# FFN of a two-layer trunk: two weight sums of a tile made one step earlier, SiLU and the gated product one step later

## The chip, the cores and the metric

The kernel runs on one core of one Trainium2 chip. Its time is the device time of one execution, in microseconds (us). The engines are TensorE (PE in the profile, with its weight loads as PEld), VectorE (DVE), ScalarE (ACT), GpSimd (POOL) and SyncE (SP), which here only issues DMAs. Each engine works through its own instructions strictly in the order in which they were written; an instruction that waits holds up all behind it on that engine.

## What is computed

A sequence of 1024 tokens of width 1024 passes two layers (a gated DeltaNet layer, then a chunked attention layer), each followed by the same kind of FFN, and a last norm. The change lies in the FFN:

```python
def conv_ffn(xn, w_up, conv_w, conv_b, w_down):
    h = causal_dwconv(xn @ w_up, conv_w) + conv_b
    gate, val = h[..., :FFN_DIM], h[..., FFN_DIM:]
    return (jax.nn.silu(gate) * val) @ w_down
```

FFN_DIM is 2816, the convolution has three taps along the sequence, and everything is in float32.

## The kernel before

**Matmuls.** A float32 product is made of three float32r matmuls: each operand is cut into a rounded high part (`h`) and the remainder, its low part (`l`), and high by high, low by high and high by low are added up in PSUM. A low part is always made in two pieces: ACT rounds (`cut_high`, L1379), then POOL or DVE subtracts (`cut_low`, through `tt`, L1358).

**Tiles of the first matrix.** `w_up` is taken in 22 tiles j of 128 gate columns and 128 value columns. With the contraction cut in halves, a tile is four blocks of weights: 11 and 12 (gate), 21 and 22 (value). It is multiplied in the manner of Strassen and Winograd: seven products of a sum of weight blocks with a sum of activation blocks, instead of eight. They run in the order 1, 7, 6, 5, 2, 4, 3. Products 1, 2 and 4 use the blocks 11, 12 and 22 as loaded. Four products need a sum of weight blocks first, made in place on DVE, each from the one before: 7: 21 = 11 − 21; 6: 21 = 21 − 22; 5: 11 = 21 + 11; 3: 12 = 12 − 21. In the profile such a sum is `r<-r,r` on DVE, the rounding is `uh<-r` on ACT, the low part `ul<-r,uh` on POOL. The activations are `x7` for product 7, `xt2` for 6, `xt1` for 5, `xt4` for 4, and `xh`, `xl` for 1, 2 and 3. The results are `pu` in PSUM. `after` (L1507 on) brings them to SBUF: `keep`, `vpre` and `gpre`.

**Convolution and gate.** `taps` makes the convolution of the value (v0, v1, v2) and of the gate (g0, g1, g2): the first tap on ACT (L1474), the two others on DVE (L1477, `val<-vpre,colt,val` and `gate<-gpre,colt,gate`). `silu` works on the gate in place on ACT (L1480, `gate<-gate`), `gated` multiplies the value by it in place on DVE (`val<-val,gate`). `hidden` cuts the result of tiles 18 to 20 into `hidh` (ACT) and `hidl` (DVE) for the last matmuls.

**The second matrix.** `w_down` is taken by nine groups g of two tiles, also by seven products each, in the order 1, 2, 5, 3, 6, 7, 4. Their weight parts are `dh` (ACT) and `dl` (POOL); the parts of the gated values ("channels") are `eh` (ACT) and `el` (DVE, or POOL in products 6 and 7). The results `pd` go to `stage` (copied by ACT, or added by DVE in products 6 and 7) and are sent to memory with an adding DMA from POOL's queue (`send`).

**The order.** All of it is written by hand. `step` appends to a list of PE steps; one step is one product, 12 matmuls. `at(i, f, rank)` puts a job ahead of step i, and the jobs of a step are emitted in order of rank. Results and `drain` have rank 0, sends 0.5, `operand` (sum, high and low part of a tile's product, two steps ahead of it) 1, the weights and channels of the second matrix (three steps ahead) 1.2 and 1.4, the convolution's pieces 2, loads 3. Two tiles and one group make 21 steps. With the products of the second matrix written d, an odd tile runs 1, 7, d5, 6, 5, d3, 2, 4, d6, 3 and an even tile 1, d7, 7, 6, d4, 5, 2, d1, 4, 3, d2. The list `when` gives the steps of the convolution: `nx(j, s)` is the s-th product of the tile after j.

```python
when[j] = [(pos[j, 7], (v0, v1), 2), (nx(j, 1), (v2, g0), 2), (nx(j, 2), (g1,), 2), (nx(j, 3), (g2, silu), 2), (nx(j, 4), (gated,), 2)]
```

Of the kernel before, what the change touches and what calls it, by code (L numbers as in the profile page):

```python
# [28 lines left out]
def trunk_kernel(  # L29
# [1323 lines left out]
    def ffn(layer, h, hp, xs, tail, d_r, last):  # L1353
# [19 lines left out]
        def at(i, f, rank=1):  # L1373

            jobs.setdefault(max(i, 0), []).append((rank, f))

        def cut_high(src, ring, copy=nc.scalar.copy):
            hi, lo = [(wd if ring == "e" else wf).tile([P, HALF], F32R, name=ring + x, tag=ring + x, bufs=RINGS[ring]) for x in "hl"]
            copy(hi, src)  # L1379
            return hi, lo  # L1380

        def cut_low(src, hi, lo, eng):
            tt(eng, lo, src, hi.bitcast(F32), sub)
# [44 lines left out]
        raw, ops = {}, {}  # L1428
# [8 lines left out]
            (nc.gpsimd if j == 0 else nc.sync).dma_start(out=t_, in_=w_up[k0 * P : (k0 + 4) * P, m * P : (m + 1) * P].rearrange("(k p) m -> p k m", p=P))  # L1437
            raw[j, q] = t_.rearrange("p k m -> p (k m)")

        def operand(j, n, lo=True):  # L1440

            a = lambda q: raw[j, q]
            if n == 7:
                tt(nc.vector, a(21), a(11), a(21), sub)
            elif n == 6:
                tt(nc.vector, a(21), a(22), a(21), sub)
            elif n == 5:
                tt(nc.vector, a(11), a(21), a(11), add)
            elif n == 3:
                tt(nc.vector, a(12), a(12), a(21), sub)  # L1450
            src = a({1: 11, 2: 12, 7: 21, 6: 21, 5: 11, 4: 22, 3: 12}[n])
            ops[j, n] = cut_high(src, "u")
            if lo:
                cut_low(src, *ops[j, n], nc.gpsimd)
            return lambda: cut_low(src, *ops[j, n], nc.vector)
# [51 lines left out]
        def after(j, n):  # L1507
            p_ = bank[j, {2: 1, 4: 7, 3: 5}.get(n, n)]
            if n == 1:
                keep[j] = tp.tile([P, HALF], F32, name="keep", tag="keep", bufs=2)  # L1510
                nc.scalar.copy(keep[j], p_)
            elif n == 6:
                tt(nc.vector, keep[j], p_, keep[j], add)
                keep[j, 7] = tp.tile([P, HALF], F32, name="keep7", tag="keep7")
                tt(nc.vector, keep[j, 7], bank[j, 7], keep[j], add)
            elif n == 5:
                tt(nc.vector, new_pre(j, 1)[:, HALF:SEQ], p_, keep[j, 7], add)
            elif n == 2:
                nc.scalar.copy(new_pre(j, 0)[:, 0:HALF], p_)
            elif n == 4:  # L1520
                tt(nc.vector, new_pre(j, 1)[:, 0:HALF], p_, keep[j], add)
            elif n == 3:
                tt(nc.vector, new_pre(j, 0)[:, HALF:SEQ], p_, keep[j], add)

        pos = {}
# [42 lines left out]
        end, fin_at = pos[FP - 1, 7], pos["d", NG - 1, 4]  # L1568
        early = pos["p", 1, 3]
        for i, (j, n) in due.items():  # L1570
            if i < early:
                low = []
                at(i - 2, lambda j=j, n=n, low=low: low.append(operand(j, n, False)), 1)
                at(i - 2, lambda low=low: low[0](), 2.5)
            else:
                at(i - 2, lambda j=j, n=n: operand(j, n), 1)
            if n != 2 or j > 2:
                at(i + 1, lambda j=j, n=n: after(j, n), 0)

        def nx(j, s):  # L1580
            return pos[j + 1, s] if j + 1 < FP else end + s
# [23 lines left out]
        for j in range(3, FP - 1):  # L1605
# [3 lines left out]
        v0, v1, v2, g0, g1, g2 = [(v, i) for v in (1, 0) for i in range(3)]  # L1609
        when = {  # L1610
            0: [(11, (g0,), 0), (12, (v0,), 0), (13, (v1,), 2), (13, (v2,), 2.7), (15, (g1, g2, silu), 2), (17, (gated,), 2)],
            1: [(18, (v0, v1), 2), (19, (v2, g0), 2), (20, (g1,), 2), (21, (g2, silu), 2), (22, (gated,), 2)],
            2: [(24, (v0, v1), 2), (25, (v2, g0), 2), (26, (g1,), 2), (27, (g2, silu), 2), (28, (gated,), 2)],
        }
        for j in range(3, FP - 1):
            when[j] = [(pos[j, 7], (v0, v1), 2), (nx(j, 1), (v2, g0), 2), (nx(j, 2), (g1,), 2), (nx(j, 3), (g2, silu), 2), (nx(j, 4), (gated,), 2)]
            if j >= 2 * NG:
                when[j].append(({18: fin_at + 5, 19: fin_at + 7}.get(j, max(nx(j, 5), fin_at + 9)), (hidden,), 1.9))
        for j, w_ in when.items():
            for i, fs, r in w_:  # L1620
                at(i, lambda j=j, fs=fs: [taps(j, *f) if isinstance(f, tuple) else f(j) for f in fs], r)
# [305 lines left out]
    d_h = [dram.tile([P, SEQ], F32, name=f"d_h{k}") for k in range(KT)]  # L1927
    xb = ([[None, None] for _ in range(KT)], [[None, None] for _ in range(KT)])
    ctx_f, tail0 = ffn(0, h, hp, normed, tails[0], d_r0, xb)
    ctx_o = ctx.enter_context(ExitStack())  # L1930
    wp = ctx_o.enter_context(tc.tile_pool(name="wp1", bufs=2, **SB))
# [288 lines left out]
    def norm_out(t, ht, fin):  # L2220
# [26 lines left out]
        return go()  # L2247

    ctx_f, _ = ffn(1, h, hp, normed, tails[0], d_r1, norm_out)
    ctx_f.close()  # L2250
    ctx_h.close()
# [56 lines left out]
```

## Time and profile before

| | us |
|---|---|
| median of three runs | 2642.77 |
| lowest and highest | 2642.44, 2644.0 |
| profiled execution | 2644.0 |
| its span, first to last instruction | 2642.0 |
| FFN of layer 0, steps of tiles | about 683 to 1314 of the span |
| FFN of layer 1, steps of tiles | about 1950 to 2584 of the span |

A row of a timeline has the start (us from the span's start), the duration, engine, line, operation and the tiles written and read; square brackets give the idle time of the engine just before and what ended it. An `x2` is two instructions told as one row. A row of the groups has busy time and mean ns, then the idle time ahead of the group and its releasers. Instructions of one engine follow each other with a little overlap in the records, and the busy time of a matmul contains its pipeline, so a row's duration is not always its price.

### The profile page before, as it was taken

How to read it: one execution, taken by the hardware profiler on the slowest of the kernel's cores; microseconds unless marked ns; L12 is line 12 of the kernel's file. 1: busy time of each engine (PE TensorE's matmuls, PEld its weight loads, DVE VectorE, ACT ScalarE, POOL GpSimd, SP SyncE). 2: the span in 40 equal slices, each digit the busy share in tenths (PEclk: the TensorE clock that was granted, in tenths of full speed). 3: DMA queues.
4: the chain of work that ended last, by engine and by line, in shares of the span. 5: the costliest groups of instructions: out<-in, count | busy, mean ns of one | idle time of the engine just before them, and what ended most of it. 6: DMA issues, size and time to landing. Idle time of an engine off the chain costs nothing.

```text
span 2642.0 us, 39392 instructions
## 1 busy us (share of the span) xinstructions
PE 2526.0 (96%) x13933; PEld 2069.7 (78%) x13933; DVE 1845.3 (70%) x3102; ACT 1409.1 (53%) x2714; POOL 1455.6 (55%) x1472
## 2 busy tenths in 40 slices
PE   7999899999999999999999999998999999999998
PEld 5878788888777777877778788887876778788776
DVE  5755765554678887888775666666478787777886
ACT  5444456464455555555455555555345555555543
POOL 3655553345347777777635444443343677777770
PEclk9999999999999999999999999999999999999999
DMA  4434335555337777777831111114232477777785
GB/s 127 137 100 121 117 105 156 159 162 160 89 88 150 141 148 151 144 143 152 191 128 50 43 58 45 45 47 143 89 95 76 132 147 141 150 147 150 151 192 176
DMA packets 317589, 326.71 MB, mean 124 GB/s; under 512 B 32976, under 2 KB 240592, under 8 KB 317392
## 3 DMA queue, kind: packets, MB, share of 16 engines
q1 hardware_dynamic: 285936, 219.07, 28.2%
q0 software_dynamic: 26560, 96.48, 20.9%
q10 hardware_dynamic: 4896, 8.65, 0.9%
q8 instruction: 109, 1.79, 0.3%
q14 instruction: 88, 0.72, 0.1%
HBM read 180.94 MB, written 143.20 MB: 123 GB/s over the span
## 4 chain that ended last, share of the span: by engine, by line
PE 47%; POOL 13%; issue 12%; DVE 12%; ACT 4%; DMA 2%; POOLq 0%; SPq 0%; ACTq 0%; DVEq 0%
POOL ul L1358 5%; PE pu L1393 5%; PE acc L120 4%; PE acc L121 4%; PE acc L122 4%; PE pu L1391 4%; PE pu L1392 4%; POOL dl L1358 3%; DVE r L1358 2%; DVE val L1477 2%; PE acco L120 2%; PE acco L122 2%; PE acco L121 2%; PE ptp L2058 2%; PE pd L1393 1%
## 5 line engine op out<-in xcount | busy, mean ns | idle before, releaser
L1358 POOL TENSOR_TENSOR ul<-r,uh 128x512 fp32r<-128x512 f32 x282 | 434.7, 1550 | 380.8 <-ACT uh L1379 362.1
L120 PE MATMUL acc<-xh,whi 128*128 128x512 f32 x896 | 376.2, 420 | 0.2 <-ACT xh L1097 0.2
L1379 ACT CAST uh<-r 128x512 fp32r<-128x512 f32 x296 | 179.9, 621 | 355.1 <-DVE r L1358 290.0
L121 PE MATMUL acc<-xl,whi 128*128 128x512 f32 x896 | 354.6, 396 | 1.6 <-POOL xl L379 1.0
L122 PE MATMUL acc<-xh,wlo 128*128 128x512 f32 x896 | 353.6, 395 | 0.6 <-POOL wlo L105 0.6
L105 POOL TENSOR_TENSOR wlo<-wraw,whi 128x256 fp32r<-128x256 f32 (+1 forms) x293 | 235.8, 836 | 199.4 <-ACT whi L103 158.2
L1393 PE MATMUL pu<-xh,ul 128*128 128x512 f32 x552 | 218.0, 395 | 16.9 <-POOL ul L1358 16.8
L1391 PE MATMUL pu<-xh,uh 128*128 128x512 f32 x552 | 216.0, 391 | 3.6 <-ACT uh L1379 2.1
L1392 PE MATMUL pu<-xl,uh 128*128 128x512 f32 x552 | 215.3, 390 | 1.0 <-POOL xl L379 1.0
L122 PEld LDWEIGHTS acc<-xh,wlo 128*128 128x128 f32 x896 | 169.5, 189 | 38.5 <-POOL wlo L105 1.0
L1358 DVE TENSOR_TENSOR r<-r,r 128x512 f32<-128x512 f32 x168 | 179.7, 1069 | 19.2 <-POOL ul L1358 19.2
L121 PEld LDWEIGHTS acc<-xl,whi 128*128 128x128 f32 x896 | 170.8, 191 | 26.0 <-POOL xl L379 3.1
L120 PEld LDWEIGHTS acc<-xh,whi 128*128 128x128 f32 x896 | 170.4, 190 | 23.1 <-ACT xh L1097 1.0
L1477 DVE SCALAR_TENSOR_TENSOR val<-vpre,colt,val 128x1023 f32<-128x1023 f32 (+2 forms) x92 | 154.9, 1683 | 38.5 <-ACT val L1474 38.4
L1700 ACT COPY stage<-pd 128x1024 f32<-128x1024 f32 x180 | 172.9, 1012 | 0.0
L2038 POOL TENSOR_SCALAR sS<-sS,st 128x640 f32<-128x640 f32 (+4 forms) x128 | 88.2, 692 | 144.1 <-DVE st L2037 124.2
L1358 DVE TENSOR_TENSOR el<-val,eh 128x512 fp32r<-128x512 f32 x90 | 99.0, 1100 | 90.8 <-ACT eh L1379 90.8
L1358 POOL TENSOR_TENSOR dl<-a,dh 128x512 fp32r<-128x512 f32 x90 | 151.9, 1688 | 18.0 <-ACT dh L1379 18.0
L1393 PEld LDWEIGHTS pu<-xh,ul 128*128 128x128 f32 x552 | 103.6, 188 | 48.6 <-POOL ul L1358 27.8
L1477 DVE SCALAR_TENSOR_TENSOR gate<-gpre,colt,gate 128x1023 f32<-128x1023 f32 (+2 forms) x92 | 134.4, 1460 | 0.2
L2036 ACT ACTIVATE sS<-sS,st 128x640 f32<-128x640 f32 (+4 forms) x128 | 89.2, 697 | 82.1 <-DVE st L2035 80.3
L1391 PEld LDWEIGHTS pu<-xh,uh 128*128 128x128 f32 x552 | 103.7, 188 | 26.1 <-ACT uh L1379 3.4
(389 smaller groups left out, 7070.6 us busy)
## 6 DMA issues: line engine op xcount, KB each, us to landing
r<-in_f_w_up_dram SPq DMA_DIRECT2D x168, 256.0 KB, 4.2
d_r<-stage POOLq DMA_DIRECT2D x78, 512.0 KB, 7.5
d_c<-stage POOLq DMA_DIRECT2D x70, 512.0 KB, 8.0
a<-in_f_w_down_dram SPq DMA_DIRECT2D x72, 256.0 KB, 2.8
wraw<-in_a_w_in_dram SPq DMA_DIRECT2D x32, 512.0 KB, 4.8
d_e<-stage POOLq DMA_DIRECT2D x32, 512.0 KB, 9.1
wraw<-in_a_w_out_dram SPq DMA_DIRECT2D x16, 512.0 KB, 4.2
d_r<-h ACTq DMA_DIRECT2D x32, 256.0 KB, 4.0
```

The source lines that it names most:

```text
L105: nc.gpsimd.tensor_tensor(lo[:, c], raw[:, c], hi[:, c].bitcast(F32), op=ALU.subtract)
L120: mm(ps, hi[:, kw, wcol : wcol + P], rh[k][s], start=st, stop=False)
L121: mm(ps, hi[:, kw, wcol : wcol + P], rl[k][s], start=False, stop=False)
L122: mm(ps, lo[:, kw, wcol : wcol + P], rh[k][s], start=False, stop=sp)
L1358: tt = lambda eng, o, a, b, op: eng.tensor_tensor(o, a, b, op=op)
L1379: copy(hi, src)
L1391: mm(ps, w[0][:, cw], x[0], start=first, stop=False, skip_group_check=True)
L1392: mm(ps, w[0][:, cw], x[1], start=False, stop=False, skip_group_check=True)
L1393: mm(ps, w[1][:, cw], x[0], start=False, stop=last, skip_group_check=True)
L1477: nc.vector.scalar_tensor_tensor(t_[:, a:c1], p_[:, a - step : c1 - step], w[:, 2 - step : 3 - step], t_[:, a:c1], op0=ALU.mult, op1=ALU.add)
L1700: nc.scalar.copy(t_, ps)
L2036: nc.scalar.activation(S, S, AF.Exp, bias=st[:, 1:2], accum_out=st[:, 2:3])
```

## The change

The four sums are taken out of `operand` into `left_sum`, which makes a sum only once. From tile 4 on, sums 5 and 3 are made right after the operands of products 6 and 4 (rank 1.05 in the same step): one product earlier, which is one or two steps. Their rounding and their low parts stay where they were. For tiles 3 to 20, `silu` moves from the step of g2 to the next product's step, at rank 1.6, which is behind the roundings of that step; `gated` moves one product further too. The rounding of tile 20's result (`hidden`) moves from `max(nx(j, 5), fin_at + 9)` to `nx(j, 6)`, one step later.

```diff
-        def operand(j, n, lo=True):
-
+        summed = set()
+
+        def left_sum(j, n):
             a = lambda q: raw[j, q]
+            if (j, n) in summed:
+                return
+            summed.add((j, n))
             if n == 7:
                 tt(nc.vector, a(21), a(11), a(21), sub)
             elif n == 6:
...
                 tt(nc.vector, a(11), a(21), a(11), add)
             elif n == 3:
                 tt(nc.vector, a(12), a(12), a(21), sub)
+
+        def operand(j, n, lo=True):
+
+            a = lambda q: raw[j, q]
+            left_sum(j, n)
             src = a({1: 11, 2: 12, 7: 21, 6: 21, 5: 11, 4: 22, 3: 12}[n])
             ops[j, n] = cut_high(src, "u")
...
                 at(i - 2, lambda j=j, n=n: operand(j, n), 1)
+                if j > 3 and n in (6, 4):
+                    at(i - 2, lambda j=j, n=n: left_sum(j, n - 1), 1.05)
...
-            when[j] = [(pos[j, 7], (v0, v1), 2), (nx(j, 1), (v2, g0), 2), (nx(j, 2), (g1,), 2), (nx(j, 3), (g2, silu), 2), (nx(j, 4), (gated,), 2)]
+            when[j] = [(pos[j, 7], (v0, v1), 2), (nx(j, 1), (v2, g0), 2), (nx(j, 2), (g1,), 2)]
+            when[j] += [(nx(j, 3), (g2,), 2), (nx(j, 4), (silu,), 1.6), (nx(j, 5), (gated,), 2)]
             if j >= 2 * NG:
-                when[j].append(({18: fin_at + 5, 19: fin_at + 7}.get(j, max(nx(j, 5), fin_at + 9)), (hidden,), 1.9))
+                when[j].append(({18: fin_at + 5, 19: fin_at + 7}.get(j, nx(j, 6)), (hidden,), 1.9))
```

## The prediction

> **What bounds the kernel now.** The page comes first: it names the engine that sets the time.
>
> ```profile
> PE 2526.0 (96%) x13933; PEld 2069.7 (78%) x13933; DVE 1845.3 (70%) x3102; ACT 1409.1 (53%) x2714; POOL 1455.6 (55%) x1472
> ```
>
> TensorE (PE) is the bound, so only the time in which it stands still can be won. Next come the stretches that the change touches, in the view by windows. The columns are the window, its length, and busy time and instruction count of PE, weight loads (PEld), DVE, ACT and POOL; then granted clock, DMA share, GB/s. The first three rows are layer 0 (tile 4, tiles 5 to 19, tiles 20 and 21), the last three layer 1.
>
> ```profile
> core 0: us, PE busy (x) PEld busy (x) DVE busy (x) ACT busy (x) POOL busy (x), PEclk, DMA share, GB/s
> 755.00:830.00 75.00, 70.33 (x298) 54.64 (x297) 60.28 (x57) 44.20 (x62) 47.72 (x39) 1.00 0.61 129
> 830.00:1258.00 428.00, 418.96 (x1825) 340.50 (x1824) 345.55 (x326) 244.52 (x349) 313.24 (x241) 1.00 0.72 145
> 1258.00:1314.00 56.00, 52.01 (x222) 40.58 (x221) 43.18 (x43) 26.32 (x38) 37.99 (x30) 1.00 0.78 168
> 2020.00:2095.00 75.00, 71.23 (x302) 55.53 (x301) 58.82 (x57) 44.48 (x63) 43.39 (x31) 1.00 0.43 127
> 2095.00:2523.00 428.00, 418.97 (x1824) 340.39 (x1823) 345.34 (x327) 244.44 (x350) 312.62 (x241) 1.00 0.72 145
> 2523.00:2584.00 61.00, 53.96 (x230) 41.81 (x230) 45.76 (x43) 27.59 (x41) 39.71 (x32) 1.00 0.85 195
> ```
>
> Busy time flatters PE, since neighbouring matmuls overlap. Their spacing is the better measure; the timeline of PE has a clean step of 12 between these two:
>
> ```profile
> 1107.19 0.39 PE L1391 MATMUL pd<-eh,dh 128*128 128x512 f32 x1
> 1109.91 0.39 PE L1391 MATMUL pu<-xt4h,uh 128*128 128x512 f32 x1
> ```
>
> That is 2.72 us a step, 0.2267 us a matmul. Length less count times 0.2267 is what PE loses: 7.4, **14.3**, 5.7 us in layer 0 and 6.5, **14.5**, 8.9 in layer 1, 57.3 us in all. The clock is 1.00 throughout, so all of it is waiting. The groups of tiles 5 to 19 in layer 0 say for what (mean ns, then the idle time ahead):
>
> ```profile
> L1393 PEld LDWEIGHTS pu<-xh,ul 128*128 128x128 f32 x172 | 32.3, 188 | 15.0 <-POOL ul L1358 8.6
> ...
> L1393 PEld LDWEIGHTS pu<-xt1h,ul 128*128 128x128 f32 x60 | 11.2, 187 | 10.8 <-POOL ul L1358 8.9
> ```
>
> PE waits for POOL's low parts of the weights (ul), under xh (products 1, 2 and 3) and under xt1h (product 5). Below, "sum n", "high n", "low n" are the DVE, ACT and POOL pieces of product n. The timelines place the waits: product 2 of an odd tile (about 0.95 us, 8 a layer), product 5 of an even one (0.85, 7 a layer), and some 0.1 for product 5 of odd tiles.
>
> **Odd tiles, product 2.** Tile 11, one fence each of DVE, ACT, POOL, PE and PEld:
>
> ```profile
> 1011.75 2.31 DVE L1477 SCALAR_TENSOR_TENSOR gate<-gpre,colt,gate 128x1022 f32<-128x1022 f32 x1
> ```
> ```profile
> 1010.69 1.92 ACT L1700 COPY stage<-pd 128x1024 f32<-128x1024 f32 x2
> 1014.16 1.06 ACT L1480 ACTIVATE gate<-gate 128x1024 f32<-128x1024 f32 x1 [1.55 <-DVE gate L1477]
> 1015.12 1.12 ACT L1379 CAST uh<-r 128x512 fp32r<-128x512 f32 x2
> ```
> ```profile
> 1015.80 1.86 POOL L1358 TENSOR_TENSOR ul<-r,uh 128x512 fp32r<-128x512 f32 x1 [2.82 <-ACT uh L1379]
> ```
> ```profile
> 1016.50 0.39 PE L1391 MATMUL pu<-xh,uh 128*128 128x512 f32 x1
> ```
> ```profile
> 1017.71 0.19 PEld L1393 LDWEIGHTS pu<-xh,ul 128*128 128x128 f32 x1 [1.02 <-POOL ul L1358]
> ```
>
> SiLU (L1480) stands in ACT's queue ahead of high 2 and waits for DVE's last tap, which ends at 1014.06. So high 2 starts at 1015.12, though ACT was free from 1012.6, and low 2 ends at 1017.66. The stall is the end of a low part less (step start + 0.27): 1017.66 − 1016.77 = 0.89. The change puts SiLU behind high 2. High 2 then starts when the stage copies end; low 2 follows more than 1 us sooner and the stall goes. SiLU still runs when the tap is there. The product with the value follows a step later, where nothing wants it before the channels of the next group. **−0.95 × 16.**
>
> **Even tiles, product 5.** Tile 12, in the same order:
>
> ```profile
> 1033.92 0.68 DVE L1358 TENSOR_TENSOR val<-val 128x512 f32<-128x512 f32 x1
> 1035.73 0.84 DVE L1358 TENSOR_TENSOR el<-val,eh 128x512 fp32r<-128x512 f32 x1 [1.13 <-ACT eh L1379]
> 1036.50 2.34 DVE L1358 TENSOR_TENSOR stage<-pd,stage 128x1024 f32<-128x1024 f32 x2
> 1038.76 1.27 DVE L1477 SCALAR_TENSOR_TENSOR gate<-gpre,colt,gate 128x1023 f32<-128x1023 f32 x1
> 1039.95 0.68 DVE L1358 TENSOR_TENSOR r<-r,r 128x512 f32<-128x512 f32 x1
> ```
> ```profile
> 1040.72 0.62 ACT L1379 CAST uh<-r 128x512 fp32r<-128x512 f32 x1 [5.02 <-DVE r L1358]
> ```
> ```profile
> 1034.74 1.29 POOL L1358 TENSOR_TENSOR ul<-r,uh 128x512 fp32r<-128x512 f32 x1 [1.46 <-ACT uh L1379]
> 1035.98 1.76 POOL L1358 TENSOR_TENSOR dl<-a,dh 128x512 fp32r<-128x512 f32 x1
> 1038.01 0.87 POOL L1715 DMA_DIRECT2D d_r<-stage  x1 [0.28 <-DVE stage L1358]
> 1039.14 0.86 POOL L1715 DMA_DIRECT2D d_r<-stage  x1 [0.26 <-DVE stage L1358]
> 1041.43 1.55 POOL L1358 TENSOR_TENSOR ul<-r,uh 128x512 fp32r<-128x512 f32 x1 [1.42 <-ACT uh L1379]
> ```
> ```profile
> 1041.87 0.39 PE L1391 MATMUL pu<-xt1h,uh 128*128 128x512 f32 x1
> ```
>
> Sum 5 is reached at 1039.95, behind two stage sums and a tap; ACT sits 5.02 us for it. Low 5 ends at 1042.98, 0.84 past 1042.14. In the changed kernel sum 5 stands ahead of the `val` at 1033.92, and high 5 is done by about 1036.5. What is late next is POOL's queue: low 5 is behind both sends, and these wait for the stage sums. Sum 5 pushes `val` by 0.6; the eh that needs it, and then el, move by 0.3 and meet low 6. With 0.4 us of delay the second send starts at 1039.55, takes 0.86, and low 5 ends at 1040.4 + 1.29 = 1041.7. That is inside 1042.14 by 0.4. **−0.85 × 14**, and the 0.1 on odd tiles goes too.
>
> **What it costs: odd tiles, product 6.** Tile 11 again, DVE, POOL, PE:
>
> ```profile
> 1005.22 0.68 DVE L1358 TENSOR_TENSOR r<-r,r 128x512 f32<-128x512 f32 x1
> 1005.83 1.27 DVE L1477 SCALAR_TENSOR_TENSOR gate<-gpre,colt,gate 128x1023 f32<-128x1023 f32 x1
> 1007.02 1.78 DVE L1358 TENSOR_TENSOR r<-r,r 128x512 f32<-128x512 f32 x1
> ```
> ```profile
> 1006.64 1.61 POOL L1358 TENSOR_TENSOR ul<-r,uh 128x512 fp32r<-128x512 f32 x1 [0.71 <-ACT uh L1379]
> ```
> ```profile
> 1008.13 0.39 PE L1391 MATMUL pu<-xt2h,uh 128*128 128x512 f32 x1
> ```
>
> These rows show a lock. Low 6 is issued at 1006.64 while DVE's tap runs to 1007.10, and takes 1.61 instead of 1.29. The sum issued at 1007.02 takes 1.78 instead of 0.68: it ends 0.55 after low 6. The two engines exclude each other and take turns. The Trainium skill has this as a rule (SBUF — State Buffer, "Who interferes with whom"): a DVE instruction with two SBUF inputs and a GpSimd one that reads SBUF block each other for the whole instruction, whoever issues second. The trace agrees, and the rule speaks against this change.
>
> For now sum 5 (1007.02) runs behind the tap. Moved, it runs at 1005.83 and the tap at 1006.43, which is 0.2 us before low 6 is issued. So low 6 waits for the tap's end at about 1007.6 and ends near 1008.9, against 1008.13 + 0.27 = 1008.40: a **new stall of 0.5 us in each odd tile, +0.5 × 16**. Bounds: 0, if low 6 gets in ahead of the tap, and 1.1, if another 0.6 us sum also passes it.
>
> Sum 3, too, gets a new wait: it overwrites block 12, which low 2 still reads. In an odd tile DVE reaches it near 1014.9 and low 2 ends near 1015.7, so it waits 0.8 us; `val`, el and the product with the gate are queued behind. They have cover, as DVE idles soon after:
>
> ```profile
> 1023.03 0.69 DVE L1358 TENSOR_TENSOR vpre<-pu,keep 128x512 f32<-128x512 f32 x1 [3.12 <-PE pu L1393]
> ```
>
> I cost it at nothing; without that cover it is 0.8 us a tile. No DMA is added or moved. The loads wait for cuts that stay where they are, so SP's queue is unchanged.
>
> **The sum.** Tiles 5 to 19: of 14.3 + 14.5 = 28.8 us lost, 16 × 0.5 = 8 comes back, a gain of 20.8. Tile 4: 7.4 + 6.5 is lost, mostly in steps whose sums don't move; its product 2 stands behind SiLU as in the odd tiles, but later. I take 1.5 a layer, 3 in all (bounds 0 and 13.9). Tiles 20 and 21: 5.7 + 8.9 = 14.6 is lost. Here sum 5 stands behind tile 18's rounding and a tap:
>
> ```profile
> 1298.17 0.68 DVE L1358 TENSOR_TENSOR r<-r,r 128x512 f32<-128x512 f32 x1
> ```
>
> It moves to about 1293.8, but the taps, gates and last weights then crowd ahead of sum 3 of tile 21. I take 9 of 14.6 (bounds 0 and 14.6). Together 32.8: the profiled execution took 2644.0 us, 2.0 more than its span; 2644.0 − 32.8 = 2611.2. It is the slowest of the three runs, 1.2 above their median, so **2610**.
>
> **The rivals.**
> - *No collision at product 6* (low 6 gets in first). For it: the margin is 0.2 us. Against: alternation as at 1007.02. 2610 − 8 = 2602, chance 0.14.
> - *The sends keep product 5 late.* If POOL starts dl before el is let in, stage sums and sends move by 1.3 us instead of 0.4, low 5 ends near 1042.9 and the even stall stays. Against: at 1035.73 el, issued during low 6, took its turn before dl. 2610 + 14 × 0.9 = 2623, chance 0.17.
> - *The sends are held by DVE.* If a send cannot be written during a tap, the second waits to 1040.3, and low 5 ends 0.35 late in 14 tiles: 2615, chance 0.05. Against: the send at 1039.14 took 0.86 beside a tap that ran from 1038.76. The Trainium skill (SBUF — State Buffer, "SBUF: two separate sides") warns that a DVE instruction in a two-port mode starves descriptor writing; the send at 1039.14 shows no sign of it.
> - *The stalls only move.* In tiles 5 to 19 DVE is busy for 345.6 and POOL for 313.2 of 428 us, partly waiting for each other. If that lock is the true limit, PE loses what it lost: 2637 to 2647, chance 0.08. High 2 and sum 5 not starting sooner although they are issued sooner belongs here.
> - *Slower.* Place: POOL in an odd tile. If low 2 ends as late as now (1017.66), then product 2's stall stays, sum 3 holds DVE 2.8 us instead of 0.8, `val` and the el of product 6 of the second matrix come about 0.8 late, and product 6 pays 0.5: 16 × 1.3 = 21 us more. If low 5 is also no sooner, only the 12 us of tiles 4, 20 and 21 stand against it: 2643 + 9 = 2652, chance 0.06. It decides from low 2 ending past about 1017.0.
>
> **How the numbers follow.** The forecast, 2610, has 0.50 (2604 to 2617 by itself). The range 2598 to 2630 takes in it, the first three rivals and most of the bounds at the ends of the layers; about 0.16 is left out. A measurement of this kernel can tell about 0.2%, or 5.3 us. Faster: 0.50 + 0.14 + 0.17 + 0.05 = 0.86; same 0.08; slower 0.06.
>
> **What the profile would show.** Right: no idle ahead of the ul load of product 2 in odd and product 5 in even tiles; high 5 of even tiles before 1037 in tile 12's time, without the 5.02; SiLU behind two high parts; a 0.5 us wait at xt2h,ul in odd tiles; windows of tiles 5 to 19 some 10 us shorter at an equal count. Wrong: idle at xt1h,ul that stays with sends ahead of it (second rival), or DVE rows waiting for POOL ul for more than 1 us ahead of sum 3 (last rival).

## The result and the profile after

| us | before | after |
|---|---|---|
| median (four runs each) | 2643.39 | 2617.19 |
| lowest and highest | 2642.44, 2648.79 | 2616.91, 2620.86 |
| span of the profiled execution | 2642.0 | 2615.1 |

The ratio is 0.990, its 95% interval 0.9883 to 0.9917: 26.2 us faster by the medians, where 32.8 had been forecast from the profiled execution. The time lies inside the range, 7 us above the point.

The first row of the page of the changed kernel, to be set against the one of before. PE's share is the same 96%, so it doesn't show the gain; DVE and POOL are busier by 17 and 30 us at equal counts of instructions; some of it is time in which one waits for the other, as tile 11 shows below.

```profile
PE 2517.5 (96%) x13933; PEld 2071.1 (79%) x13933; DVE 1862.1 (71%) x3102; ACT 1413.1 (54%) x2714; POOL 1485.5 (57%) x1472
```

Next the view by windows of the changed kernel, cut as in the prediction: tile 4, tiles 5 to 19, tiles 20 and 21 of each layer. The window edges follow the tiles, which come sooner now; the windows of the last tiles are as long as before. The names are rough: the window of tile 4 holds all of tile 3 but its first product, and that of tiles 20 and 21 begins in tile 19, with product 6 of the second matrix.

```profile
core 0: us, PE busy (x) PEld busy (x) DVE busy (x) ACT busy (x) POOL busy (x), PEclk, DMA share, GB/s
751.00:826.00 75.00, 71.01 (x299) 54.74 (x298) 63.44 (x58) 45.34 (x64) 50.34 (x39) 1.00 0.65 137
826.00:1242.00 416.00, 414.61 (x1819) 340.26 (x1817) 351.56 (x325) 243.90 (x346) 323.14 (x240) 1.00 0.72 148
1242.00:1298.00 56.00, 51.92 (x215) 41.11 (x216) 43.90 (x41) 27.93 (x40) 39.77 (x30) 0.97 0.81 179
2003.00:2078.00 75.00, 72.04 (x308) 56.81 (x307) 56.51 (x58) 45.26 (x64) 45.48 (x32) 1.00 0.44 133
2078.00:2495.00 417.00, 416.62 (x1831) 342.61 (x1830) 351.37 (x326) 244.18 (x347) 325.59 (x241) 1.00 0.72 148
2495.00:2556.00 61.00, 55.94 (x227) 44.02 (x226) 50.01 (x46) 30.52 (x44) 41.97 (x32) 0.94 0.90 210
```

Length less matmuls times 0.2267 us, the measure of the prediction, gives what PE loses:

| us lost, both layers | before | after | gain | forecast |
|---|---|---|---|---|
| tile 4 | 7.4 + 6.5 | 7.2 + 5.2 | 1.5 | 3 |
| tiles 5 to 19 | 14.3 + 14.5 | 3.6 + 1.9 | **23.3** | 20.8 |
| tiles 20 and 21 | 5.7 + 8.9 | 7.3 + 9.5 | **−2.2** | 9 |

Together 22.6. The other 4 us of the 26.9 by which the spans differ have nothing to do with the change: well ahead of the first FFN the profiled execution of before was granted less than the full clock for a while (0.90 over 51 us), as the same stretch of both shows (windows of before, then of after).

```profile
270.00:321.00 51.00, 45.21 (x207) 37.25 (x206) 37.81 (x108) 25.30 (x79) 25.31 (x35) 0.90 0.38 111
```
```profile
266.00:317.00 51.00, 43.16 (x216) 35.85 (x217) 40.86 (x115) 25.30 (x79) 25.07 (x35) 1.00 0.44 123
```

**Tiles 5 to 19.** The groups of the changed kernel in the window of layer 0 that the prediction used (830 to 1258; mean ns, then the idle time ahead and what ended it):

```profile
L1393 PEld LDWEIGHTS pu<-xh,ul 128*128 128x128 f32 x180 | 33.8, 188 | 7.2 <-POOL ul L1358 0.2
...
L1393 PEld LDWEIGHTS pu<-xt2h,ul 128*128 128x128 f32 x59 | 11.1, 187 | 5.7 <-POOL ul L1358 3.5
...
L1393 PEld LDWEIGHTS pu<-xt1h,ul 128*128 128x128 f32 x56 | 10.5, 188 | 2.2
```

The 8.6 us of waiting for low parts under xh are down to 0.2, and the 8.9 under xt1h have left no trace. New are 3.5 us under xt2h, which had none: product 6. Tile 11 shows all three (DVE, ACT, POOL and PEld of the changed kernel):

```profile
993.65 1.41 DVE L1358 TENSOR_TENSOR r<-r,r 128x512 f32<-128x512 f32 x2
994.97 1.28 DVE L1486 SCALAR_TENSOR_TENSOR gate<-gpre,colt,gate 128x1023 f32<-128x1023 f32 x1
```
```profile
1002.01 0.63 ACT L1379 CAST uh<-r 128x512 fp32r<-128x512 f32 x1
1002.54 1.07 ACT L1489 ACTIVATE gate<-gate 128x1024 f32<-128x1024 f32 x1
```
```profile
995.07 4.03 POOL L1358 TENSOR_TENSOR ul<-r,uh 128x512 fp32r<-128x512 f32 x2 [0.71 <-ACT uh L1379]
...
1002.72 1.30 POOL L1358 TENSOR_TENSOR ul<-r,uh 128x512 fp32r<-128x512 f32 x1
```
```profile
997.44 0.19 PEld L1393 LDWEIGHTS pu<-xt2h,ul 128*128 128x128 f32 x1 [0.49 <-POOL ul L1358]
```

Sums 6 and 5 run back to back at 993.65, the gate tap behind them from 994.97, and low 6 is issued at 995.07, 0.1 us later: it waits for the tap's end and then works, so that the two low parts take 4.03 us. PE's weights wait 0.49 us. SiLU (L1489) stands behind high 2 now, low 2 is issued at 1002.72, and product 2, which starts at 1005.31, waits for nothing.

**The end of a layer** has become worse. In layer 0 of the changed kernel, PE's row shows what its longest wait is for, and DVE's rows what stands ahead of it:

```profile
1291.27 0.76 PE L1391 MATMUL pu<-xt4h,uh 128*128 128x512 f32 x1 [2.77 <-DVE keep L1358]
```
```profile
1285.08 1.35 DVE L1358 TENSOR_TENSOR fl<-fr,fh 128x512 fp32r<-128x512 f32 x1 [2.04 <-ACT fh L1788]
1286.36 1.21 DVE L1358 TENSOR_TENSOR hidl<-val,hidh 128x1024 fp32r<-128x1024 f32 x1
1287.49 2.30 DVE L1486 SCALAR_TENSOR_TENSOR gate<-gpre,colt,gate 128x1022 f32<-128x1022 f32 x1
1289.72 1.40 DVE L1358 TENSOR_TENSOR keep<-pu,keep 128x512 f32<-128x512 f32 x2
```

Product 4 of tile 21 waits for `keep`, the sum that takes a result out of PSUM, and `keep` stands behind weights for the last matmuls (`fl`), the low part of tile 19's result (`hidl`) and tile 20's last gate tap. The load of block 12 has a part in it. In layer 0 it was issued at 1268.72 and landed 15.1 us later; ACT's rounding for product 2 starts at 1283.91 (the profile puts the 4.30 us ahead of it down to PE, but the landing falls 0.1 us before), `fh` follows it on ACT, and DVE stands still for 2.04 us until `fh` is there. In layer 1 ACT waits for that load for 4.93 us, and DVE then 3.23 us for `hidh` behind it (ACT, rounding for product 2):

```profile
2541.38 0.62 ACT L1379 CAST uh<-r 128x512 fp32r<-128x512 f32 x1 [4.93 <-DMA r<-in_f_w_up_dram]
```

Two of the clock's rows of the changed kernel lie there too, and a third stretch at 0.50 lasts from 2550.5 to 2553.9; in before the clock was 1.00 throughout both ends:

```profile
1292.00:1294.00 2.00, 2.00 (x7) 1.52 (x6) 1.34 (x2) 1.95 (x4) 1.28 (x1) 0.50 0.51 151
...
2544.00:2547.00 3.00, 3.00 (x9) 2.32 (x8) 3.00 (x2) 0.62 (x1) 2.81 (x2) 0.50 1.06 327
```

And tile 19 has a wait that before did not have, 1.65 and 1.39 us at product 6 of the last group of the second matrix. DVE and POOL there:

```profile
1235.90 3.91 DVE L1358 TENSOR_TENSOR r<-r,r 128x512 f32<-128x512 f32 x1 [2.12 <-POOL ul L1358]
1239.74 0.68 DVE L1358 TENSOR_TENSOR val<-val 128x512 f32<-128x512 f32 x1
```
```profile
1235.14 1.56 POOL L1734 DMA_DIRECT2D d_r<-stage  x1
1235.75 2.27 POOL L1358 TENSOR_TENSOR ul<-r,uh 128x512 fp32r<-128x512 f32 x1
1237.01 2.25 POOL L1358 TENSOR_TENSOR dl<-ay,dh 128x512 fp32r<-128x512 f32 x1
```

Sum 3, early now, takes 3.91 us instead of 0.68: POOL makes two low parts one after the other without letting it in. The `val` behind it starts at 1239.74, and with it the channels of that product 6 come late (`el`, on POOL, starts at 1241.15, and product 6 at 1242.03).

### The profile page after: what moved, and what is told of

It is laid out like the page before. It is cut to its first block, busy times and chain, and to the rows that moved or that the text cites. A ratio compares the mean times of both kernels' runs of the same rounds, so it can differ in the third digit from the quotient of the medians.

```text
span 2615.1 us, 39396 instructions
## 1 busy us (share of the span) xinstructions
PE 2517.5 (96%) x13933; PEld 2071.1 (79%) x13933; DVE 1862.1 (71%) x3102; ACT 1413.1 (54%) x2714; POOL 1485.5 (57%) x1472
## 4 chain that ended last, share of the span: by engine, by line
PE 53%; POOL 5%; DVE 5%; issue 3%; ACT 2%; DMA 2%; DVEq 0%; POOLq 0%; ACTq 0%; SPq 0%
PE pu L1393 8%; PE pu L1391 8%; PE pu L1392 8%; PE pd L1392 4%; PE pd L1393 4%; PE pd L1391 4%; PE acc L120 3%; PE acc L121 3%; PE acc L122 3%; POOL ul L1358 2%; PE ptp L2070 2%; PE poT L2100 1%; PE poT L2099 1%; PE acco L120 1%; PE acco L121 1%
## 5 line engine op out<-in xcount | busy, mean ns | idle before, releaser
L1358 POOL TENSOR_TENSOR ul<-r,uh 128x512 fp32r<-128x512 f32 x282 | 445.7, 1600 | 297.6 <-ACT uh L1379 276.2
L1486 DVE SCALAR_TENSOR_TENSOR gate<-gpre,colt,gate 128x1023 f32<-128x1023 f32 (+2 forms) x92 | 175.4, 1906 | 0.8
L1358 DVE TENSOR_TENSOR r<-r,r 128x512 f32<-128x512 f32 x168 | 131.5, 782 | 31.0 <-POOL ul L1358 29.6
L1392 PEld LDWEIGHTS pu<-xl,uh 128*128 128x128 f32 x552 | 104.2, 189 | 23.6 <-POOL xl L379 2.1
```

Source lines behind the costliest of these rows:

```text
L1358: tt = lambda eng, o, a, b, op: eng.tensor_tensor(o, a, b, op=op)
L1392: mm(ps, w[0][:, cw], x[1], start=False, stop=False, skip_group_check=True)
L1486: nc.vector.scalar_tensor_tensor(t_[:, a:c1], p_[:, a - step : c1 - step], w[:, 2 - step : 3 - step], t_[:, a:c1], op0=ALU.mult, op1=ALU.add)
```

## The experiments

All were timed in five rounds against the kernel before on the same chip (its medians there: 2643.28 to 2643.75); the versions were spread over four chips, so the ratios compare better than the medians. "Wait" in the tables is by step: what PE's matmul starts are apart, over 0.2267 us each, summed over the named steps, from the profiled execution of each version. Matmuls at half clock count in it as well; steps that lose under 0.05 us are left out, and product 6 of the second matrix in tile 19 is in the second table alone. The sums hold to about 0.2 us. The diffs are against the changed kernel unless said.

### The parts one by one

**SiLU alone moved.** The sums stay where they were.

```diff
-                if j > 3 and n in (6, 4):
-                    at(i - 2, lambda j=j, n=n: left_sum(j, n - 1), 1.05)
```

> Only SiLU, the gated product and tile 20's rounding are moved; all sums stay with their operands. Theory (the two stalls are separate): the wait of product 2 in odd tiles (0.95 us, 16 of them) and most of that of tile 4 (3 us) go, product 5 of even tiles keeps its 0.85, product 6 of odd tiles gets no new wait: about 18 us less than before, 2625. Rival (the shared lock of DVE and POOL is the limit, stalls only move): less than 8 us of gain, with waits at other products.

**The sums alone ahead.** The list `when` is that of before.

```diff
-            when[j] += [(nx(j, 3), (g2,), 2), (nx(j, 4), (silu,), 1.6), (nx(j, 5), (gated,), 2)]
+            when[j] += [(nx(j, 3), (g2, silu), 2), (nx(j, 4), (gated,), 2)]
```

> Only sums 5 and 3 are made ahead; SiLU and the gated product stand as before. Theory: product 5 of even tiles loses its 0.85 (14 of them) and tile 20 its 1.5 twice, 15 us in all; product 6 of odd tiles gets 0.36 (16 of them), 6 us; product 2 of odd tiles keeps its 0.95; the end of each layer loses some 2 us: 7 to 9 us less than before, 2635. Rival (the gain of the whole change comes from the sums): 20 us or more.

**Sum 5 ahead in even tiles only.**

```diff
-                if j > 3 and n in (6, 4):
+                if j > 3 and (n == 4 or n == 6 and j % 2 == 0):
```

> The changed kernel, but sum 5 is made ahead in even tiles only. Theory (in odd tiles it pushes the gate's tap past the issue of low part 6, and the lock then costs 0.36): the waits at product 6 of odd tiles go, 0.1 at product 5 of some odd tiles comes back: 4 us faster than the changed kernel, 2613. Rival (product 6 waits for its own sum or its rounding): the same time as the changed kernel, the waits of 0.36 still there.

**Sum 3 not ahead** (sum 5 is).

```diff
-                if j > 3 and n in (6, 4):
+                if j > 3 and n == 6:
```

> The changed kernel, but sum 3 stays with its operand in all tiles. Theory (in tile 19 the early sum 3 is held for 3.9 us by POOL, and the channels of the last product 6 of the second matrix queue behind it): the 1.65 and 1.39 there go, nothing is lost in tiles 5 to 18: 2 to 3 us faster than the changed kernel, 2614; tile 21 may lose 1 at product 3. Rival (that stall is the sends' doing, whatever DVE's order): the stall stays, same time.

**Sum 3 only ahead** (sum 5 is not).

```diff
-                if j > 3 and n in (6, 4):
+                if j > 3 and n == 4:
```

> The changed kernel without the early sum 5: SiLU and product moved, sum 3 ahead. Theory: the 0.9 us at product 5 of even tiles stay (14 x 0.9 = 13 us), the 0.36 us at product 6 of odd tiles go (6 us less), so 2617 + 13 - 6 = about 2624, the same as with SiLU alone moved (2623.7): sum 3 is worth something only where sum 5 is ahead as well. Rival: sum 3 ahead is worth its 9 us by itself (what the kernel lost when it alone was put back): about 2615.

| version | median us | ratio to before (95%) | wait, tiles 5 to 19, two layers | of it product 2 odd, 5 even, 6 odd |
|---|---|---|---|---|
| before | 2643.39 | | 14.6, 14.7 | 15.4, 11.8, 0 |
| SiLU alone | 2623.65 | 0.9918 (0.9905 to 0.9932) | 7.9, 6.4 | 0, 13.3, 0.2 |
| SiLU, sum 3 | 2628.76 | 0.9943 (0.9930 to 0.9955) | 8.9, 8.8 | 0, 17.4, 0 |
| SiLU, sum 5 | 2626.71 | 0.9933 (0.9921 to 0.9946) | 7.7, 5.8 | 0, 0, 12.6 |
| SiLU, both sums (the change) | 2617.19 | 0.9900 (0.9883 to 0.9917) | 3.2, 2.2 | 0, 0, 5.2 |
| SiLU, sum 3, sum 5 in even tiles | 2618.48 | 0.9904 (0.9891 to 0.9918) | 4.0, 3.8 | 0, 0.3, 0 |
| both sums alone | 2658.53 | 1.0062 (1.0049 to 1.0075) | 22.2, 21.8 | 0.1, 0.3, 15.2 |

The first expectation held: SiLU behind high 2 alone ends the wait of product 2, and is worth 19.6 us. The groups under xh and xt1h of that kernel, in the same window, show one wait gone and the other left:

```profile
L1393 PEld LDWEIGHTS pu<-xh,ul 128*128 128x128 f32 x180 | 33.8, 188 | 7.0
...
L1393 PEld LDWEIGHTS pu<-xt1h,ul 128*128 128x128 f32 x60 | 11.3, 188 | 10.2 <-POOL ul L1358 8.1
```

Of the rest most missed, and what they missed is the better lesson: **the parts don't add up**. Without SiLU's move, the sums make the kernel 15 us slower, where 8 us of gain was expected. On top of SiLU's move neither sum alone gains anything: with sum 3 the kernel is 5.1 us slower by the medians (the intervals touch), with sum 5 3.1 (they overlap). Both together are 6.5 us faster by the medians; here too the intervals overlap, but the waits of tiles 5 to 19 fall from 14.3 to 5.4 us.

The loss of the sums alone can be read in tile 10 of that kernel (DVE, ACT, PEld):

```profile
978.14 3.71 DVE L1486 SCALAR_TENSOR_TENSOR gate<-gpre,colt,gate 128x1023 f32<-128x1023 f32 x2
```
```profile
981.95 1.06 ACT L1489 ACTIVATE gate<-gate 128x1024 f32<-128x1024 f32 x1 [6.52 <-DVE gate L1486]
982.92 0.60 ACT L1379 CAST uh<-r 128x512 fp32r<-128x512 f32 x1
```
```profile
984.93 0.19 PEld L1393 LDWEIGHTS pu<-xh,ul 128*128 128x128 f32 x1 [1.07 <-POOL ul L1358]
```

Product 5 starts on time there, at 980.58, and so product 2 is due 0.85 us sooner than it used to be. But high 2 still stands behind SiLU, SiLU behind the second gate tap, and that tap now meets low 5: the two taps take 3.71 us. Product 2 waits about 1.3 us in even tiles (9.0 us a layer over tiles 5 to 19), where it had waited for nothing: the stall of product 5 had been its cover. The wait of product 2 in odd tiles is gone too, but product 6 pays about 1 and product 7 another 0.39 in nearly each of them. So the stall of product 5 has only moved, as the fourth rival of the prediction had it, until SiLU gets out of the way.

Sum 5 in even tiles only shows the new stall of product 6 to be the collision that the prediction described: with sum 5 of odd tiles back behind the gate tap, the 5.2 us at product 6 of odd tiles are gone. What still waits under xt2h is the even tiles' product 6.

The time stays the same (2618.48 and 2617.19 with overlapping intervals). DVE and POOL collide at other products for about as much: 0.2 us at product 6 of even tiles, 0.1 to 0.3 at product 5 of odd ones, and 1.2 us in layer 0 at product 1 of the second matrix.

Without the early sum 3, 2614 was expected, 2 to 3 us less. Its absence costs 9.5 us instead. The step at which this appears is product 6 of odd tiles, 0.6 to 1.0 us in nearly all of them, 0.33 on average in the changed kernel. DVE there:

```profile
994.71 2.31 DVE L1486 SCALAR_TENSOR_TENSOR val<-vpre,colt,val 128x1022 f32<-128x1022 f32 x1
996.95 1.40 DVE L1358 TENSOR_TENSOR r<-r,r 128x512 f32<-128x512 f32 x2
```

That kernel's product 6 is due at 999.56, so sum 6 begins 2.6 us ahead of it; in the changed kernel it begins at 993.65 for a product due at 996.76, 3.1 us ahead. DVE's queue is the same up to there, but it runs 0.5 us later relative to PE. POOL and DVE show where it lost that, first without the early sum 3, then in the changed kernel:

```profile
987.65 1.94 POOL L1358 TENSOR_TENSOR ul<-r,uh 128x512 fp32r<-128x512 f32 x1
988.16 2.52 DVE L1486 SCALAR_TENSOR_TENSOR val<-vpre,colt,val 128x1023 f32<-128x1023 f32 x1 [1.31 <-ACT val L1483]
```
```profile
984.37 1.92 POOL L1358 TENSOR_TENSOR ul<-r,uh 128x512 fp32r<-128x512 f32 x1
985.37 2.02 DVE L1486 SCALAR_TENSOR_TENSOR val<-vpre,colt,val 128x1023 f32<-128x1023 f32 x1 [1.31 <-ACT val L1483]
```

Product 7 starts at 994.12 and 991.32, so the value's tap is issued equally early in both, 5.96 and 5.95 us ahead of it. But low 1 of the new tile is issued 0.5 us later (6.5 instead of 7.0 us ahead), and the tap, which runs only when low 1 is done, takes 2.52 us instead of 2.02. Low 1 is later because POOL's work in front of it is: that begins with low 3 of the tile before, which starts 0.8 us later when its sum is not made ahead.

### The end of the layers

**Block 12 of tile 21 loaded two products earlier**, into a second buffer.

```diff
-... bufs=1 if tag == "r12" or tag[0] == "a" else 2)
+... bufs=1 if tag[0] == "a" else 2)
-                at(pos[j, s], lambda j=j, q=q: load(j + 1, q), 3)
+                at(pos[j, 5 if (j, q) == (FP - 2, 12) else s], lambda j=j, q=q: load(j + 1, q), 3)
```

> The changed kernel, with the gate block 12 of tile 21 loaded two products earlier, into a second buffer. Theory: tile 21's product 2 waits (1.21 us in layer 0, 4.35 in layer 1) because this load lands 15 to 16 us after its issue instead of 6 to 7; and the long gaps there bring the half clock that follows (about 5 us in both layers). So these waits go, product 4 of tile 21 gets back some of it, and the kernel takes about 2610 (7 us less than the changed kernel's 2617). Rival: the channels and low parts of tile 21 come late by themselves, so that product 4 takes over what product 2 loses: 2615 to 2619, no change.

**The sums from tile 19 on as before.**

```diff
-                if j > 3 and n in (6, 4):
+                if 3 < j < 19 and n in (6, 4):
```

> The changed kernel, but the sums are ahead only in tiles 4 to 18; tiles 19 to 21 make them where the kernel before did. Theory: at the end of a layer the early sums do harm, since there they run into sends, and what follows comes late together; with SiLU alone moved, tiles 20 and 21 lose 4.9 and 8.4 us in the two layers, where the changed kernel loses 8.3 and 10.0 with tile 19, and no half clock follows. So the sum of waits falls by about 5 us and the half clock's 5 us go: about 2609. Rival: the end is late through whatever precedes it (tiles 5 to 18 run 15 us sooner, so that loads and sends of the end are more crowded), not through its own sums: 2615 to 2619.

**The rounding of tile 19's result two steps later**, with block 12 early.

```diff
-... {18: fin_at + 5, 19: fin_at + 7} ...
+... {18: fin_at + 5, 19: fin_at + 9} ...
```

> The kernel with block 12 early, and the rounding of tile 19's result (hidh, hidl) two steps later, behind the keep of tile 21 (the same work, later in the queues of ACT and DVE). Theory: product 4 of tile 21 needs the PSUM that keep frees, and keep stands on DVE behind hidl (2.31 us) and a gate tap (2.29 us), each taking turns with POOL. Without hidl ahead of it, keep comes 2.3 us sooner in each layer, product 4's wait falls from 5.85 to about 3.5, and less half clock follows: 2617.6 - 4.6 - up to 3 = 2610 to 2613. Rival: POOL's low parts (2.25 us each there, back to back) are what is late, so that the wait moves to low 4 or product 3: 2615 to 2619.

**The same, and no early sums in tile 19.**

```diff
-                if j > 3 and n in (6, 4):
+                if j > 3 and j != 19 and n in (6, 4):
```

> The same as the last, with tile 19 alone making its sums where the kernel before did. Theory: the wait at product 6 of the last group of the second matrix (1.65 and 1.37 us) comes from tile 19's own early sums, which run into the sends of the total behind which POOL keeps the turn; it falls below 0.3 a layer, some 2.5 us in all, so 2608 to 2611. Rival: tile 19 then pays 0.9 us at product 2 or elsewhere as odd tiles did in the kernel before, or the end takes it back: no gain over the last kernel.

**The gate tap behind `keep` as well** (against the last but one).

```diff
+            z = j == FP - 2
-... [(nx(j, 3), (g2,), 2), (nx(j, 4), (silu,), 1.6), (nx(j, 5), (gated,), 2)]
+... [(nx(j, 3 + z), (g2,), 2), (nx(j, 4 + z), (silu,), 1.6), (nx(j, 5 + z), (gated,), 2)]
-... .get(j, nx(j, 6))
+... .get(j, nx(j, 7))
```

> The first of these three, with the last gate tap, SiLU, product and rounding of tile 20 one step later too, so that keep of tile 21 stands behind neither hidl nor the tap. Theory (DVE's queue ahead of keep is the bound): keep another 2.3 us sooner, product 4's wait falls to about 1 us, and no half clock follows; but the tail gets tile 20's result one step later, of which it may pay 1 us: 2604 to 2609. Rival: the tail waits for the result of tile 20 and gives all of it back: 2612 to 2617.

**The rounding of tile 19's result later, alone**, with block 12 where it was.

> The changed kernel with only the rounding of tile 19's result two steps later; block 12 of tile 21 is loaded where it was. Theory: there are two chains to tile 21's product 4, one through the late load (product 2's wait of 1.21 and 4.35 us) and one through DVE's queue ahead of keep, and the later one decides. With the load's left in place, product 2's wait stays, and less than the 4.8 us is won that the same edit won with the load early: 2614 to 2617. Rival: DVE's queue alone counts and the load is harmless: 2612 to 2613, as with both edits.

**Block 12 early, rounding later, no early sums in tile 19, sum 5 ahead in even tiles only.**

> The version with block 12 early, tile 19's rounding later and no early sums in tile 19 (2611.4), with sum 5 ahead in even tiles only. Theory: the collision at product 6 of odd tiles goes (2.7 and 1.9 us), but, as when sum 5 alone was taken back in odd tiles, the waits at product 5 of odd and product 6 of even tiles that come instead (3.7 and 3.6 us there, with d1) eat it: 2609 to 2613. Rival: with the end repaired, the gain shows: 2605 to 2608.

| version | median us | ratio to before (95%) | wait from tile 19's product 6 of the second matrix on, two layers | of it tile 21's products 2 and 4 |
|---|---|---|---|---|
| before | 2643.39 | | 6.1, 9.6 | 0 and 5.9 |
| the change | 2617.19 | 0.9900 (0.9883 to 0.9917) | 8.3, 10.0 | 5.6 and 7.9 |
| block 12 early | 2617.62 | 0.9903 (0.9890 to 0.9917) | 8.9, 8.3 | 0 and 11.7 |
| old sums from 19 | 2617.59 | 0.9899 (0.9884 to 0.9914) | 5.4, 11.8 | 1.6 and 5.9 |
| block 12 early, rounding later | 2612.81 | 0.9882 (0.9866 to 0.9899) | 5.5, 3.8 | 0 and 4.6 |
| the same, no sums in 19 | 2611.44 | 0.9873 (0.9858 to 0.9888) | 2.4, 6.2 | 0 and 6.1 |
| block 12 early, rounding and tap later | 2616.66 | 0.9897 (0.9883 to 0.9912) | 2.0, 6.8 | 0 and 1.0 |
| rounding later alone | 2614.51 | 0.9891 (0.9876 to 0.9905) | 3.3, 5.9 | 4.1 and 1.4 |
| all together, sum 5 even only | 2617.06 | 0.9905 (0.9888 to 0.9921) | 4.1, 3.8 | 0 and 1.4 |

The early load settles that the load alone is not what bounds the end: product 2's waits went, and product 4 took over most of them, as the rival had it. DVE no longer stands still ahead of `fl` and of tile 19's `hidl`, but its queue meets POOL's low parts instead (`hidl` takes 2.31 us for 1.21). With block 12 early, PE and DVE of layer 0:

```profile
1296.43 0.77 PE L1391 MATMUL pu<-xt4h,uh 128*128 128x512 f32 x1 [3.35 <-DVE keep L1358]
```
```profile
1290.44 2.31 DVE L1358 TENSOR_TENSOR hidl<-val,hidh 128x1024 fp32r<-128x1024 f32 x1
1292.67 2.29 DVE L1486 SCALAR_TENSOR_TENSOR gate<-gpre,colt,gate 128x1022 f32<-128x1022 f32 x1
1294.88 1.40 DVE L1358 TENSOR_TENSOR keep<-pu,keep 128x512 f32<-128x512 f32 x2
```

Taking `hidl` out of that queue won 4.8 us over this kernel by the medians, as expected (the intervals overlap at the edge, but the wait that was to fall fell from 11.7 to 4.6). Most of that fall is the clock: standing still ahead of product 4 fell only from 3.35 and 3.36 us to 2.86 and 1.14, but with block 12 early alone 6.8 us at 0.50 lie at the end of each layer, and here none. How far that holds for the other runs isn't shown: from run to run of one version the granted clock of the whole execution moves by 0.002 to 0.004, and 0.001 of 2610 us is 2.6 us. The same two engines with the rounding later, in layer 1, and the window of its end, granted at full clock:

```profile
2545.72 0.47 PE L1391 MATMUL pu<-xt4h,uh 128*128 128x512 f32 x1 [1.14 <-DVE keep L1358]
```
```profile
2539.70 4.54 DVE L1486 SCALAR_TENSOR_TENSOR gate<-gpre,colt,gate 128x1023 f32<-128x1023 f32 x2
2544.17 1.40 DVE L1358 TENSOR_TENSOR keep<-pu,keep 128x512 f32<-128x512 f32 x2
```
```profile
2510.00:2570.00 60.00, 57.72 (x264) 46.15 (x263) 45.52 (x48) 29.30 (x44) 34.16 (x25) 1.00 1.01 261
```

So **DVE's queue ahead of `keep` is what bounds product 4**, and the last step confirms it: with the gate tap behind `keep` too, product 4 waits for nothing in layer 0 and 1 us in layer 1. But it is not all of the end. The tap now stands ahead of the next sum out of PSUM, and product 3 loses 3.9 us in layer 1 to that one, 2.12 of them in standing still and the rest mostly at half clock behind it (PE and DVE of that kernel):

```profile
2548.89 0.77 PE L1391 MATMUL pu<-xh,uh 128*128 128x512 f32 x1 [2.12 <-DVE vpre L1358]
```
```profile
2545.82 2.32 DVE L1486 SCALAR_TENSOR_TENSOR gate<-gpre,colt,gate 128x1022 f32<-128x1022 f32 x1
2548.06 0.68 DVE L1358 TENSOR_TENSOR vpre<-pu,keep 128x512 f32<-128x512 f32 x1
```

That kernel is no faster (3.9 us slower by its median, with overlapping intervals). The waits are about as long in sum (8.8 and 9.3 us): the wait has moved by one product. That the tail pays for tile 20's later result, as the rival had it, isn't shown. From the last matmul of layer 1's tiles to the end of the span it is 60.1 us in both kernels, and the stretch between the layers, 637.7 and 636.2 us, is anywhere from 631.8 to 639.5 us in the versions here. Of the rounding later alone (2614.51), the times don't tell whether the late load matters beside it: its interval overlaps that of the version with the load early. By its trace the load still costs 4.1 us at product 2 in layer 1, and product 4 then waits for nothing.

Old sums from tile 19 on gave nothing: the waits of layer 0 fell by 2.9 us, those of layer 1 rose by 1.8. But the wait at product 6 of the second matrix in tile 19 does come from tile 19's own early sums: 1.63 and 1.41 us with them, 0.21 and under 0.05 without. POOL holds DVE for as long there, only it is `val` that is held, not a sum ahead of it, so that `val` is done at 1238.26 and not at 1240.42 (the two kernels enter tile 4 within 0.4 us of each other):

```profile
1234.36 3.90 DVE L1358 TENSOR_TENSOR val<-val 128x512 f32<-128x512 f32 x1
```

In the time this is 1.4 us between two kernels with overlapping intervals, so not shown to be a gain. The last version, all together, gave no more (2617.06).

The fastest versions, 2612.81 and 2611.44, beat the kernel before by 31 to 32 us. Over the changed kernel the gain is 4.4 and 5.8 us by the medians; the intervals of the first overlap with its own, those of the second by little.

## Why the prediction was right, and where it was wrong

**Product 2 of odd tiles (−0.95 × 16): right, and for the reason given.** The wait is gone in all odd tiles up to 19; SiLU alone does it.

**Product 5 of even tiles (−0.85 × 14): right** in the changed kernel, where it is gone in tiles 6 to 20. But the 0.85 us were put down as the yield of sum 5 by itself. Sum 5 ends that wait with or without SiLU's move (0.3 us are left in the sums alone), yet time is won only with SiLU's move and sum 3 beside it: the sums without SiLU cost 15 us. The prediction added the edits up in the changed order and gave no thought to which of them depends on which. That the sum for tiles 5 to 19 came out (23.3 for 20.8) is in part luck, since it rests on sum 3, which the prediction took to be worth nothing.

**The new stall at product 6 of odd tiles (+0.5 × 16): the right place and mechanism, the size a little high.** It is 0.33 us on average by PE's spacing (5.2 us in 16 tiles instead of 8; up to 0.55, and nothing in two of them). The margin was as thin as the prediction had it: the tap is issued 0.1 us ahead of low 6 (0.2 forecast). The rule that it took from the Trainium skill (SBUF — State Buffer, "Who interferes with whom"), a lock held for the whole instruction, agrees: low 6, the first of the two at 995.07, takes 2.33 us where it took 1.61.

**Sum 3 at nothing: wrong.** Its wait in odd tiles is there (0.49 us ahead of the `r` at 1004.06, 0.8 forecast) and costs nothing, as the prediction said. But the prediction saw no worth in the early sum. Beside sum 5 it is worth 9.5 us by the medians; 7.4 us of waiting at product 6 of odd tiles go with it, since sum 6 starts 0.5 us sooner ahead of its product.

**The other rivals.** The sends did not keep product 5 late, and DVE did not hold them: in tile 10 the second send takes 0.94 us beside a gate tap, and product 5 starts on time. The mechanism of *slower* did not occur, low 2 being issued 2.6 us ahead of product 2. *The stalls only move* is what happens with the sums alone.

**Tile 4: 1.5 for 3**, within its bounds. By steps tile 4 itself lost 4.2 and 2.7 us before and 3.3 and 1.9 after; the rest of that window's 13.9 us is mostly tile 3's, which the change hardly touches. Product 2 of tile 4 gained 3.1 us in both layers together, and product 6 gave 1.4 back.

**Tiles 20 and 21 (9 of 14.6): the step that failed.** The prediction saw that "the taps, gates and last weights then crowd", and took 9 us all the same; it came to −2.2. What it priced did leave. By steps, in both layers together, product 5 of tile 20 lost 3.0 us and now loses nothing, product 5 of tile 21 went from 4.0 to 0.7 and product 3 from 2.5 to 0.4. What it did not price came to more: 3.0 us at product 6 of the second matrix in tile 19, 5.6 at product 2 of tile 21 and 2.0 more at product 4. It left out the queue that stays, DVE's `fl`, `hidl` and tap ahead of `keep`: when the weights come sooner, PE arrives at tile 21 sooner, and waits there for a PSUM bank that comes no sooner. It also took the loads as unchanged ("SP's queue is unchanged"), and block 12 of tile 21 landed 15.1 and 16.0 us after its issue instead of 5.8 and 6.9. And it had no term for POOL keeping DVE out in tile 19. Its bound, 0, was not low enough.

The clock is part of it. In the windows of the ends of the changed kernel it is 0.97 and 0.94; missing shares of 0.03 of 56 us and 0.06 of 61 make up to 5.3 us of the 16.8 lost there. Without these, by this estimate, the ends would have gained some 3 us of the 9, not lost 2. The prediction counted on a clock of 1.00, as in before. About the wait of 2.77 us that ends at 1291.27 the clock falls to 0.50. The Trainium skill (TensorE: Matmul & The Clock Gate, Part 1) has the clock halve after an idle window of some 3.4 us; the trace shows it halved at shorter waits too, as PE's rows ahead of the stretch at 2544 have it:

```profile
2542.05 0.50 PE L1391 MATMUL pu<-xh,uh 128*128 128x512 f32 x1 [1.57 <-ACT uh L1379]
...
2543.41 0.60 PE L1393 MATMUL pu<-xh,ul 128*128 128x512 f32 x1 [0.63 <-POOL ul L1358]
```

The length of a wait alone does not decide it. One of 2.12 us brought 0.50 in layer 1 of the version with the tap later; one of 3.41 us (product 4 in layer 1 of SiLU alone) and one of 2.86 (layer 0 of block 12 early, rounding later) left the clock at 1.00.

## What to carry to other kernels

Before you add up the gains of two edits, ask of each what it is worth without the other: a stall that you remove can be the cover of the next chain, and here the one that looked like half the gain was a loss until the other was there. At the end of a loop, look for what frees the buffers (here a sum out of PSUM behind work that nobody waits for yet) rather than at what feeds the engine. Where two engines lock each other out, the order of their instructions matters by tenths of a microsecond, and here taking away one collision mostly made another.

## What was not expected of the hardware

DVE and POOL take turns in most places, but not in all: behind a send issued on POOL's queue, POOL made two low parts of 2.27 and 2.25 us in a row while a DVE sum was pending, which then took 3.91 us, and with that tile's sums put back a `val` took 3.90 in the same place. In the even tiles 6 to 18 the last gate tap, 1.27 us where nothing is in its way, takes 4.8 to 5.3 us behind two sends, 4.91 in tile 10, where POOL makes three low parts meanwhile; no product of tile 10 waits for it. Why the turn isn't given was not tried.

A load can land much later beside the adding sends: block 12 of tile 21, 256 KB, landed 15.1 us after its issue in layer 0 of the changed kernel (before, 5.8). The sends were about as busy in both, in 81.5% of the engines' time from 1268 to 1284 us and, in the kernel before, in 83.7% from 1287 to 1297. But in a microsecond of steady sends (1282 to 1283) the loads moved 0.02 MB, and in one in which the sends paused 0.33 (1292 to 1293 of the kernel before, 5 us after the issue there). So the landing seems to hang on whether a pause follows the issue; this is read from the views and was not tried.

The half clock behind waits of 1.6 to 2.8 us was the third surprise. It did not come at the ends of SiLU alone or of the version with block 12 early and the rounding later, where the clock is 1.00; what decides between these cases stays open.
